# A two-layer hybrid block on one core: rests of split weights kept in DRAM, and the planner's price for a change of the array's shape

## The chip, the cores and the metric

The kernel runs on one core of a Trainium2 chip. The metric is the device time of one execution in microseconds, of which several runs are taken. A core has TensorE (PE in the profile, with its weight loads as PEld), VectorE (DVE), ScalarE (ACT), GpSimd (POOL) and SyncE (SP), which here issues all DMAs from one queue, in order.

## What is computed

Two layers over 1024 tokens of width 1024. Each layer has an input projection, three mixers side by side (an attention over the 256 best keys by an index score, an RWKV-7 recurrence, a sparse attention with compressed, selected and windowed keys), an output projection and a gated feed-forward network:

```python
for l in range(DEPTH):                       # DEPTH = 2, B = 1, T = 1024, D = 1024
    h = rms_norm(x, norm1_g[l]) * (1.0 + sc1) + sh1
    z = h @ w_in[l]
    ...
    o_a, o_b, o_c = dsa_mixer(...), rwkv7_mixer(...), nsa_mixer(...)
    mixed = jnp.concatenate([o_a, o_b, o_c], axis=-1) @ w_out[l]
    x = x + g1 * mixed
    h = rms_norm(x, norm2_g[l]) * (1.0 + sc2) + sh2
    gate, up = jnp.split(h @ ffn_wi[l], 2, axis=-1)
    x = x + g2 * ((jax.nn.silu(gate) * up) @ ffn_wo[l])
```

sh1, sc1, g1, sh2, sc2, g2 are six vectors of a linear map of the condition c (tensor `ada_w`). All is float32.

## The kernel before

The tokens are worked on in two halves of 512 (h = 0 and 1). A stage D(l, h) is the input projection of layer l for half h, a stage F(l, h) its output projection and feed-forward network; the main stream runs D00, D01, F00, D10, F01, D11, F10, F11 (the digits are l and h). The mixers' work runs beside them in streams of their own, and fills PE between the dense matmuls.

**Split weights.** PE multiplies in fp32r, and each product of float32 matrices is made of three: with weights and activations split into a rounded part and a rest, hi x hi, hi x lo and lo x hi (function `dense`, with activations named hh/hl, ohi/olo, acthi/actlo). A weight item is 128 partitions x 512 columns, 256 KB: four blocks of 128x128, so 12 matmuls over 512 tokens (a few items, of `wo`, have half of it). `Feed` hands the items out: 50 for a D stage, 152 for an F stage, 808 in all. For each, SP loads `wraw`, ACT rounds it to `whi`, and POOL subtracts to give the rest, `wlo` (`split`). Both halves of the tokens use the same weights, and both load and split them anew. `Feed.ahead` keeps two items split and up to two raw ones loaded. The tiles wraw, whi and wlo come from one pool of eight slots (`w=8`).

In this kernel's slots a raw load takes the slot of the raw item two before it, which comes free when POOL has subtracted that one; whi and wlo take the slots of the item three before, free when PE has done its last matmul on them.

**The order.** Nothing is scheduled while the kernel runs. `trace` is run once to record all operations with their dependences (`Program.add`); `Program.order` then places them one by one on the five engines by a table of costs (`Chip`), always the operation that can start first, and of several that are ready on one engine the one that was recorded first. Engines run their lists in the order that this gives. PE has one more rule: its 128x128 array can also work as smaller arrays ("shapes", counted in units of 32 rows and 32 columns, the full one being (4, 4)). `Chip.is_part` tells only full from partial; if the next matmul is of the other kind than the one before, and one of the same kind is ready that was recorded at most LATER = 100 operations after it, that one goes first. `Chip.start` and `Chip.put` price a change from full to partial with 0.095 + 0.05 us and one back with 0.045 + 0.105 us, and a change between two partial shapes with nothing.

On SP, DMAs go out in the planned order, each after the waits of its own; one that waits holds up all behind it.

Each instruction shows in the profile at L697, where `Program.issue` emits it, so tiles rather than lines tell operations apart. S, po, Y, X and at are tiles of the mixers: S, Y and X of the RWKV units, at and po of attention. z, k, v, r, low, dg, inv and Tt in DMAs are tiles that RWKV units pass through DRAM.

Of the kernel before, what the change touches and what calls it, by code (L numbers as in the profile page):

```python
# [13 lines left out]
F32 = mybir.dt.float32  # L14
# [483 lines left out]
class Rec:  # L498
    __slots__ = ("key", "name", "a", "k", "cost", "deps", "n", "users", "pe", "func", "port", "prio")
# [21 lines left out]
class Program:  # L521
# [32 lines left out]
    def add(self, key, name, a, k, aps, outs, cost, pe=None, port=False):  # L554
# [3 lines left out]
        r.prio = self.weave.cur.prio  # L558
# [46 lines left out]
    def order(self):  # L605
# [5 lines left out]
        kinds, begun = ([], []), set()  # L611
# [11 lines left out]
        while len(out) < len(recs):  # L623
            best = None
            for e in ENGINES:
                t = chip.free[e]
                if not ready[e]:
                    if not coming[e]:
                        continue
                    t = max(t, coming[e][0][0])  # L630
                while coming[e] and coming[e][0][0] <= t:
                    n = heapq.heappop(coming[e])[1]
                    heapq.heappush(ready[e], n)
                    if e == "PE":
                        heapq.heappush(kinds[Chip.is_part(recs[n])], n)
                n = ready[e][0]
                if e == "PE" and Chip.is_part(recs[n]) != chip.part:
                    same = kinds[chip.part]
                    while same and same[0] in begun:
                        heapq.heappop(same)  # L640
                    if same and same[0] - n <= LATER:
                        n = same[0]
                s = max(chip.start(recs[n]), at[n])
                if s > t + 0.1 and recs[n].port:

                    for m in heapq.nsmallest(8, ready[e])[1:]:
# [56 lines left out]
class Chip:  # L703
# [5 lines left out]
    def __init__(self):  # L709
        self.free = {e: 0.0 for e in ENGINES}  # L710
        self.cells = [[0.0] * 4 for _ in range(4)]
        self.part, self.first = False, False
        self.port, self.wire, self.table, self.ring = 0.0, 0.0, None, [0.0] * 8
        self.stretch, self.work, self.over, self.slow, self.lost = 0, 0.0, 0.0, False, 0.0

    @staticmethod
    def is_part(r):
        rows, cols, _ = r.pe
        return rows[1] - rows[0] + cols[1] - cols[0] < 8

    def start(self, r):

        t = self.free[r.key]
        if r.key == "PE":
            rows, cols, _ = r.pe
            part = self.is_part(r)
            for i in range(*rows):
                t = max(t, max(self.cells[i][cols[0]:cols[1]]))
            return t + (0.0 if part == self.part else 0.095 if part else 0.045)
# [4 lines left out]
    def put(self, r, s):  # L734

        if r.key == "PE":
# [6 lines left out]
            part = self.is_part(r)  # L743
            more = 0.105 if not part and self.first else 0.0

            step = c if not part or r.a[1].dtype != F32 else c / 2 + (0.0 if self.first else 0.05)
            if part and cols[1] - cols[0] == 1:
                step = 0.014
            self.first = part
# [8 lines left out]
            self.part = part  # L758
# [32 lines left out]
def trace(ctx: ExitStack, tc: tile.TileContext, A, out, layers=L, plan=None, program=None):  # L791
# [34 lines left out]
    def nm(s):  # L826
        cnt[0] += 1
        return f"{s}_{cnt[0]}"
# [101 lines left out]

    class Feed:


        def __init__(self, items):
            self.items, self.raw, self.split = list(items), [], []

        def load(self, n):
            while len(self.raw) < n and self.items:
                src, w, *led = self.items.pop(0)
# [5 lines left out]
                self.raw.append((raw, w, bool(led)))  # L945

        def ahead(self, n=AHEAD):
            self.load(1)
            while len(self.split) < n and self.raw:
                raw, w, led = self.raw.pop(0)  # L950
                self.split.append(split(raw, w, "w", G))
# [1466 lines left out]
    feed = Feed([i for k, l, h in seq for i in (items_D(l, h) if k == "D" else items_F(l, h))])  # L2418
# [106 lines left out]
```

## Time and profile before

| | us |
|---|---|
| median of 3 runs | 3439.8 |
| lowest and highest of them | 3438.86, 3444.59 |
| the profiled execution | 3442.73 |
| its span in the trace | 3441.0 |
| PE busy | 3215.3 |
| DVE busy | 2176.2 |
| ACT busy | 1775.1 |
| POOL busy | 1488.3 |

The busy time of an engine is the union of its instructions' times. Matmuls are pipelined: one of 512 columns is shown as some 0.4 us long, and the next one starts 0.23 us later. Where an engine sat idle, the view of waits names what ended the idle time. The stages overlap at their edges; here a stage is taken to begin when ACT splits its first weight item.

### The profile page before, as it was taken

To read this page: it belongs to the slowest core of one execution; us is meant where nothing else is said; L and a number is where in the kernel's file an instruction comes from. 1 tells how busy PE (TensorE), PEld (TensorE's weight loads), DVE (VectorE), ACT (ScalarE), POOL (GpSimd) and SP (SyncE) were. 2 spreads that over 40 slices of the span, in tenths; PEclk is the share of its full clock that TensorE was granted. 3 is DMA by queue.
4 is the path that set the end of the run, shared out by engine and by line. 5 is a ranking of instruction groups with operands and counts; after the bars stand their busy time and mean duration, and the time that the engine had idled before them with its cause. 6 is when DMAs were issued, how large, how long until landed. Compare 5 with 4: busy or idle time off the path is not lost. (4 is left out here: it accounts for less than half of the span.)

```text
span 3441.0 us, 58566 instructions
## 1 busy us (share of the span) xinstructions
PE 3215.3 (93%) x20564; PEld 2496.7 (73%) x20564; DVE 2176.2 (63%) x5705; ACT 1775.1 (52%) x3706; POOL 1488.3 (43%) x1235
## 2 busy tenths in 40 slices
PE   6898999989999998889899999899799999999999
PEld 3656776767767776767678887677577787778887
DVE  4688988898899634698952114698888853241112
ACT  3445566756674643545464234567777454343232
POOL 2433453434335444442434554443343344445554
PEclk8999999989999998999899999899999999999999
DMA  8684345445523243554223333463232222423333
GB/s 280 197 260 124 108 138 160 145 138 161 194 77 108 70 131 113 154 157 118 74 67 115 98 97 114 145 189 122 67 86 67 84 80 80 144 91 96 98 95 98
DMA packets 354755, 424.99 MB, mean 124 GB/s; under 512 B 129686, under 2 KB 167190, under 8 KB 354460
## 3 DMA queue, kind: packets, MB, share of 16 engines
q1 hardware_dynamic: 354460, 421.25, 39.9%
q8 instruction: 162, 2.65, 0.3%
q14 instruction: 133, 1.09, 0.1%
HBM read 347.06 MB, written 60.44 MB: 118 GB/s over the span
## 5 line engine op out<-in xcount | busy, mean ns | idle before, releaser
L697 POOL TENSOR_TENSOR wlo<-wraw,whi 128x512 fp32r<-128x512 f32 (+1 forms) x808 | 1072.1, 1329 | 1346.1 <-ACT whi L697 1243.1
L697 ACT ACTIVATE whi<-wraw 128x512 fp32r<-128x512 f32 (+1 forms) x808 | 500.7, 622 | 993.9 <-PE mm L697 664.6
L697 PE MATMUL mm<-hh,whi 128*128 128x512 f32 x2144 | 865.9, 405 | 38.5 <-ACT hh L697 10.4
L697 PE MATMUL mm<-hh,wlo 128*128 128x512 f32 x2128 | 847.9, 399 | 5.5 <-POOL wlo L697 5.4
L697 PE MATMUL mm<-hl,whi 128*128 128x512 f32 x2112 | 843.7, 400 | 5.5 <-DVE hl L697 3.2
L697 PEld LDWEIGHTS mm<-hh,whi 128*128 128x128 f32 x2144 | 410.5, 192 | 141.2 <-issue 16.1
L697 PEld LDWEIGHTS mm<-hh,wlo 128*128 128x128 f32 x2128 | 407.1, 191 | 101.0 <-POOL wlo L697 10.1
L697 PEld LDWEIGHTS mm<-hl,whi 128*128 128x128 f32 x2112 | 404.3, 191 | 94.6 <-issue 8.2
L697 DVE TENSOR_TENSOR sg<-sg,mm 128x512 f32<-128x512 f32 x87 | 59.5, 684 | 474.0 <-PE mm L697 473.8
L697 DVE SCALAR_TENSOR_TENSOR x<-mm,mod,x 128x512 f32<-128x512 f32 x232 | 172.9, 747 | 245.5 <-PE mm L697 244.5
L697 PE MATMUL mm<-acthi,whi 128*128 128x512 f32 x704 | 280.4, 402 | 13.9 <-DVE x L697 5.8
L697 PE MATMUL mm<-actlo,whi 128*128 128x512 f32 x704 | 277.6, 397 | 1.9 <-POOL actlo L697 1.8
L697 PE MATMUL mm<-acthi,wlo 128*128 128x512 f32 x704 | 276.6, 396 | 0.0
L697 ACT ACTIVATE p<-p,nb,rst 128x512 f32<-128x512 f32 (+3 forms) x256 | 170.6, 667 | 62.0 <-DVE nb L697 60.7
L697 ACT ACTIVATE junka<-score,tk_nt 128x512 int8<-128x512 f32 x240 | 165.9, 691 | 21.5 <-DVE tk_nt L697 16.0
L697 PEld LDWEIGHTS mm<-acthi,whi 128*128 128x128 f32 x704 | 133.3, 190 | 49.8 <-DVE x L697 6.8
L697 ACT COPY pT<-pt 128x512 f32<-128x512 f32 (+2 forms) x220 | 121.8, 588 | 70.3 <-PE pt L697 50.4
L697 PEld LDWEIGHTS mm<-actlo,whi 128*128 128x128 f32 x704 | 133.4, 190 | 31.2 <-POOL actlo L697 6.7
L697 PEld LDWEIGHTS mm<-acthi,wlo 128*128 128x128 f32 x704 | 133.5, 190 | 27.4 <-issue 0.2
L697 DVE TENSOR_SCALAR p<-p,rs 128x512 f32<-128x512 f32 (+3 forms) x288 | 151.9, 579 | 1.5 <-issue 0.9
L697 PE MATMUL pt<-c_ident,p 128*128 128x128 f32 x816 | 134.9, 282 | 14.3 <-DVE p L697 6.7
L697 PEld LDWEIGHTS pt<-c_ident,p 128*128 128x128 f32 x816 | 100.9, 143 | 48.8 <-issue 11.8
(386 smaller groups left out, 5916.7 us busy)
## 6 DMA issues: line engine op xcount, KB each, us to landing
wraw<-in_wi_dram SPq DMA_DIRECT2D x352, 256.0 KB, 2.6
ada<-in_ada_dram SPq DMA_DIRECT2D x192, 256.0 KB, 4.4
wraw<-in_win_dram SPq DMA_DIRECT2D x184, 256.0 KB, 3.2
wraw<-in_wo_dram SPq DMA_DIRECT2D x160, 256.0 KB, 2.6
x<-x SPq DMA_DIRECT2D x64, 256.0 KB, 3.7
w<-in_w_dram SPq DMA_DIRECT2D x64, 256.0 KB, 3.8
wraw<-in_wout_dram SPq DMA_DIRECT2D x64, 256.0 KB, 2.8
o_in<-o SPq DMA_DIRECT2D x32, 256.0 KB, 3.5
```

The lines of the kernel that those rows point to most:

```text
L697: getattr(engines[r.key], r.name)(*[real(x) for x in r.a], **{n: real(x) for n, x in r.k.items()})
```

## The change

Two things change.

First, `Feed` keeps the rests of three pairs of stages: ("D", 0), ("F", 0) and ("D", 1). In the first half's stage (D00, F00, D10) each wlo that POOL has made is also written to a DRAM tile of its own, by a DMA on SP. In the second half's stage (D01, F01, D11) the item's rest is loaded from there into a slot of the same pool, right behind its raw weights; ACT still rounds whi, and POOL subtracts nothing. F10 and F11 are as before. An item with a loaded rest counts twice in the limit of what is loaded ahead. There are 252 such items: 252 writes and 252 loads are new, and 252 of the 808 subtractions go. By the slots, a raw load of the second half's three stages now mostly takes the slot of the wlo four items before, which is free after PE's last matmul on it, and a load of a rest takes the slot of the raw item before, which is free after ACT's split.

Second, the planner tells the shapes of the array apart (`shape_of` in place of `is_part`): a change between any two shapes is priced with 0.095 us, and with 0.05 more on the first matmul in a partial shape or 0.105 on the first in the full one; and the rule of LATER now prefers a ready matmul of the very shape that PE is in.

```diff
-        kinds, begun = ([], []), set()
+        kinds, begun = {}, set()
...
-                        heapq.heappush(kinds[Chip.is_part(recs[n])], n)
+                        heapq.heappush(kinds.setdefault(Chip.shape_of(recs[n]), []), n)
                 n = ready[e][0]
-                if e == "PE" and Chip.is_part(recs[n]) != chip.part:
-                    same = kinds[chip.part]
+                if e == "PE" and Chip.shape_of(recs[n]) != chip.shape:
+                    same = kinds.get(chip.shape)
...
     @staticmethod
-    def is_part(r):
+    def shape_of(r):
         rows, cols, _ = r.pe
-        return rows[1] - rows[0] + cols[1] - cols[0] < 8
+        return rows[1] - rows[0], cols[1] - cols[0]
...
-            return t + (0.0 if part == self.part else 0.095 if part else 0.045)
+            return t + (0.0 if self.shape_of(r) == self.shape else 0.095)
...
-            part = self.is_part(r)
-            more = 0.105 if not part and self.first else 0.0
-
-            step = c if not part or r.a[1].dtype != F32 else c / 2 + (0.0 if self.first else 0.05)
+            shape = self.shape_of(r)
+            part, changed = shape != (4, 4), shape != self.shape
+            more = 0.105 if changed and not part else 0.0
+
+            step = c if not part or r.a[1].dtype != F32 else c / 2
+            if part and changed:
+                step += 0.05
...
+    KEPT = {("D", 0), ("F", 0), ("D", 1)}
...
         def load(self, n):
-            while len(self.raw) < n and self.items:
-                src, w, *led = self.items.pop(0)
+
+            while self.items:
+                (kind, l, h), src, w, *led = self.items[0]
+                if self.raw and sum(1 + (x[1] is not None) for x in self.raw) + 1 + (h and (kind, l) in KEPT) > n:
+                    break
+                self.items.pop(0)
                 raw = slot("wraw")
...
                 SY.dma_start(dst, src)
-                self.raw.append((raw, w, bool(led)))
+                key = lo = None
+                if (kind, l) in KEPT:
+                    key = src.tensor.name, src.offset
+                    if h:
+                        lo, key = slot("wlo", F32R), self.rests.pop(key)
+                        SY.dma_start(lo.bitcast(F32)[:, :w], key[:, :w])
+                self.raw.append((raw, lo, key, w, bool(led)))
...
-                raw, w, led = self.raw.pop(0)
-                self.split.append(split(raw, w, "w", G))
+                raw, lo, key, w, led = self.raw.pop(0)
+                if lo is not None:
+                    hi = slot("whi", F32R)
+                    S.activation(hi[:, :w], raw[:, :w], AF.Copy)
+                    self.split.append((hi, lo))
+                else:
+                    self.split.append(split(raw, w, "w", G))
+                    if key:
+                        t = self.rests[key] = dram(nm("rest"))
+                        SY.dma_start(t[:, :w], self.split[-1][1].bitcast(F32)[:, :w])
```

The planner puts the operations of all five engines in another order, nearly everywhere. Three places show what kind of change it is. The first is PE early in F01, before, where two RWKV units (S, Y: arrays of 64x64 and 128x64) and an attention block (po: 128x64) stand between dense matmuls (mm):

```order
L697 MATMUL mm_18411<-ohi_16782,wlo_18247 128x512
L697 MATMUL S_18154<-sh_18170,MT_18069 64x64 x2
L697 MATMUL po_17758<-pT_18369,tm_14168 64x256 x2
L697 MATMUL S_18332<-sh_18356,MT_18300 64x64 x2
L697 MATMUL S_18154<-sh_18170,MT_18069 64x64 x2
L697 MATMUL po_17758<-pT_18377,tm_14168 64x256 x2
L697 MATMUL Y_18448<-UV_17043,A_17115 64x64
L697 MATMUL Y_18448<-UV_17057,A_17131 64x64
L697 MATMUL S_18332<-sh_18356,MT_18300 64x64 x2
```

PE early in F01 after the change, with the same kinds of matmuls:

```order
L697 MATMUL mm_18929<-olo_17315,whi_18772 128x512
L697 MATMUL S_18945<-S_4853,MT_18846 64x64 x2
L697 MATMUL S_18640<-sh_18647,MT_18581 64x64 x2
L697 MATMUL po_18294<-pT_18871,tm_14346 64x256 x2
L697 MATMUL po_18294<-pT_18898,tm_14346 64x256 x2
L697 MATMUL S_18945<-sh_18952,MT_18846 64x64 x2
L697 MATMUL S_18640<-sh_18647,MT_18581 64x64 x2
L697 MATMUL mm_18929<-ohi_17207,wlo_18543 128x512
```

Matmuls of one shape from different units now stand together. The second place is SP late in D10, before:

```order
L697 DMA z10k_16948<-z_16901 128x512
L697 DMA k_16978<-z10k_16948 128x512
L697 DMA wraw_16983<-in_win_dram 128x512
L697 DMA wraw_17034<-in_win_dram 128x512
L697 DMA wraw_17053<-in_win_dram 128x512
L697 DMA z10v_17059<-z_17002 128x512
L697 DMA v_17099<-z10v_17059 128x4x64 x2
```

SP at the same place after the change:

```order
L697 DMA k_17215<-z10k_17180 128x512
L697 DMA rest_17225<-wlo_17202 128x512
L697 DMA wraw_17231<-in_win_dram 128x512
L697 DMA z10v_17234<-z_17198 128x512
L697 DMA v_17276<-z10v_17234 128x4x64 x2
L697 DMA rest_17292<-wlo_17245 128x512
L697 DMA wraw_17296<-in_win_dram 128x512
```

A write of a rest stands ahead of each raw load. The third is SP in F01, before, where w are weights of the compression and o results of attention:

```order
L697 DMA wraw_21181<-in_wi_dram 128x512
L697 DMA w_5429_21193<-in_w_dram 128x128
L697 DMA o_20606<-o_21191 128x128
L697 DMA o_20610<-o_21191 128x128
L697 DMA wraw_21219<-in_wi_dram 128x512
L697 DMA wraw_21237<-in_wi_dram 128x512
```

SP in F01 after the change, where an RWKV unit's Tt is loaded between:

```order
L697 DMA wraw_20123<-in_wi_dram 128x512
L697 DMA wlo_20126<-rest_9768 128x512
L697 DMA Tt_20118<-inv_414 64x8x64
L697 DMA wraw_20134<-in_wi_dram 128x512
L697 DMA wlo_20148<-rest_9821 128x512
L697 DMA wraw_20214<-in_wi_dram 128x512
L697 DMA wlo_20224<-rest_9922 128x512
```

Each raw load has the load of its rest behind it.

## Rows read from the trace of the kernel before

**Rows 1.** The page: the span, and busy time by engine.

```profile
span 3441.0 us, 58566 instructions
PE 3215.3 (93%) x20564; PEld 2496.7 (73%) x20564; DVE 2176.2 (63%) x5705; ACT 1775.1 (52%) x3706; POOL 1488.3 (43%) x1235
```

**Rows 2.** Windows: length, PE, PEld, DVE, ACT, POOL busy, clock, DMA share, GB/s.

```profile
34.80:311.50 276.70, 244.48 (x1562) 171.25 (x1562) 201.81 (x619) 128.01 (x277) 113.12 (x93) 0.93 0.68 209
311.50:662.30 350.80, 326.45 (x2686) 248.27 (x2684) 307.13 (x847) 218.12 (x494) 147.80 (x130) 0.97 0.46 135
662.30:1330.90 668.60, 629.16 (x4219) 487.49 (x4219) 499.02 (x1284) 392.12 (x845) 282.57 (x229) 0.97 0.41 127
1330.90:1551.50 220.60, 190.29 (x1043) 148.29 (x1043) 163.49 (x424) 105.17 (x212) 107.01 (x84) 0.92 0.48 143
1551.50:2127.10 575.60, 554.70 (x3761) 444.74 (x3760) 273.57 (x721) 248.77 (x495) 255.87 (x216) 0.98 0.32 97
2127.10:2357.90 230.80, 207.51 (x1112) 160.83 (x1111) 184.12 (x449) 145.01 (x309) 105.12 (x83) 0.93 0.51 157
...
3007.60:3441.00 433.40, 420.45 (x1876) 343.46 (x1876) 105.34 (x148) 141.76 (x236) 212.29 (x167) 0.99 0.30 96
```

**Rows 3.** Timeline of PE in F01: start us, us, engine, matmul, x count.

```profile
1612.19 0.45 PE L697 MATMUL S<-sh,MT 64*64 64x64 f32 x8
1612.57 0.65 PE L697 MATMUL po<-pT,tm 128*64 128x256 f32 x4
...
1613.27 0.33 PE L697 MATMUL S<-sh,MT 64*64 64x64 f32 x4
1613.53 0.33 PE L697 MATMUL Y<-UV,A 128*64 128x64 f32 x2
```

**Rows 4.** Waits of PE, 0 to 312 us: total us, times, longest.

```profile
PE mm L697 <- ACT whi L697: 3.8, 2, 2.3
PE mm L697 <- POOL wlo L697: 3.1, 2, 2.4
```

**Rows 5.** Waits of PE in D01, F01 and D11 (one view each).

```profile
PE X L697 <- DVE ex L697: 4.6, 1, 4.6
...
PE bc L697 <- DVE ex L697: 3.4, 2, 1.9
...
PE mm L697 <- DVE z L697: 6.4, 1, 6.4
PE mm L697 <- ACT whi L697: 4.0, 1, 4.0
```

**Rows 6.** Timelines of DVE and of POOL (last row), in D01.

```profile
484.20 0.75 DVE L697 SCALAR_TENSOR_TENSOR score<-rl,tm,score 128x512 f32<-128x512 f32 x1
...
485.93 1.15 DVE L697 TENSOR_SCALAR rx<-gv 128x8 f32<-128x8 f32 x1
487.00 1.86 DVE L697 SCALAR_TENSOR_TENSOR score<-rl,tm,score 128x512 f32<-128x512 f32 x1
...
485.77 2.54 POOL L697 TENSOR_TENSOR wlo<-wraw,whi 128x512 fp32r<-128x512 f32 x2 [3.14 <-ACT whi L697]
```

**Rows 7.** Feed: a group, timelines of POOL, SP and ACT, a DMA's landing.

```profile
L697 POOL TENSOR_TENSOR wlo<-wraw,whi 128x512 fp32r<-128x512 f32 (+1 forms) x808 | 1072.1, 1329 | 1346.1 <-ACT whi L697 1243.1
...
2999.77 0.33 SPq L697 DMA_DIRECT2D wraw<-in_wout_dram  x1
3300.70 1.29 POOL L697 TENSOR_TENSOR wlo<-wraw,whi 128x512 fp32r<-128x512 f32 x1 [1.42 <-ACT whi L697]
3302.02 14.01 SPq L697 DMA_DIRECT2D wraw<-in_wo_dram  x6
3302.71 0.63 ACT L697 ACTIVATE whi<-wraw 128x512 fp32r<-128x512 f32 x1 [2.09 <-PE mm L697]
3305.43 0.63 ACT L697 ACTIVATE whi<-wraw 128x512 fp32r<-128x512 f32 x1 [1.60 <-PE mm L697]
...
wraw<-in_wi_dram SPq DMA_DIRECT2D x352, 256.0 KB, 2.6
```

More of the change, by code (lines that the diff above doesn't have):

```diff
@@ L498 @@
 class Rec:
-    __slots__ = ("key", "name", "a", "k", "cost", "deps", "n", "users", "pe", "func", "port", "prio")
+    __slots__ = ("key", "name", "a", "k", "cost", "deps", "n", "users", "pe", "func", "port", "prio", "scope")
 def spread(offset, dims, unit):
@@ L557, in add @@
         r.n, r.deps, r.users = len(self.recs), set(), []
-        r.prio = self.weave.cur.prio
+        r.prio, r.scope = self.weave.cur.prio, self.weave.cur.scope
         r.func = a[2] if key == "S" and name == "activation" else None
@@ L711, in __init__ @@
         self.cells = [[0.0] * 4 for _ in range(4)]
-        self.part, self.first = False, False
+        self.shape = 4, 4
         self.port, self.wire, self.table, self.ring = 0.0, 0.0, None, [0.0] * 8
@@ L742, in put @@
                 self.stretch += 1
-            part = self.is_part(r)
-            more = 0.105 if not part and self.first else 0.0
-            step = c if not part or r.a[1].dtype != F32 else c / 2 + (0.0 if self.first else 0.05)
+            shape = self.shape_of(r)
+            part, changed = shape != (4, 4), shape != self.shape
+            more = 0.105 if changed and not part else 0.0
+            step = c if not part or r.a[1].dtype != F32 else c / 2
+            if part and changed:
+                step += 0.05
             if part and cols[1] - cols[0] == 1:
                 step = 0.014
-            self.first = part
             share = 1.0 if not part else (rows[1] - rows[0]) * (cols[1] - cols[0]) / 16.0
@@ L757, in put @@
                     self.cells[i][cols[0]:cols[1]] = [s + c + more] * (cols[1] - cols[0])
-            self.part = part
+            self.shape = shape
             self.free["PE"] = s + step + more
@@ L929, in drain @@
             pass
+    KEPT = {("D", 0), ("F", 0), ("D", 1)}
     class Feed:
         def __init__(self, items):
-            self.items, self.raw, self.split = list(items), [], []
+            self.items, self.raw, self.split, self.rests = list(items), [], [], {}
         def load(self, n):
-            while len(self.raw) < n and self.items:
-                src, w, *led = self.items.pop(0)
+            while self.items:
[3 more added lines that the diff above has]
+                self.items.pop(0)
                 raw = slot("wraw")
@@ L2417, in trace @@
                 seq.append(("D", l + 1, h))
-    feed = Feed([i for k, l, h in seq for i in (items_D(l, h) if k == "D" else items_F(l, h))])
+    feed = Feed([(s, *i) for s in seq for i in (items_D(*s[1:]) if s[0] == "D" else items_F(*s[1:]))])
     PR = dict(**{} or dict(index=1, topk=0, cmp=2, att=2, rw=3, rw2=4, lora=2, mod=7, main=8))
```

## The prediction

> **What bounds the kernel now.** I read the page first, then the windows by stage, then PE's waits stretch by stage, then the timelines of single engines. [rows 1] has PE busy for 3215.3 of 3441.0 us, DVE for 2176.2, ACT for 1775.1 and POOL for 1488.3. [rows 2] splits this by stage (order of the work: D00, D01, F00, D10, F01, D11, F10, F11; F10 is left out). In each stage PE is short of the stage's length by little: 32 us in D00, 24 in D01, 39 in F00, 30 in D10, 21 in F01, 23 in D11, 13 in F11. POOL is never above half of a stage, so the 252 subtractions that the change takes from it don't bound anything by themselves. DVE is 307 of 351 us in D01 and 184 of 231 us in D11: there it is nearly as full as PE. The granted clock (a mean of its two levels, 2.4 and 1.2 GHz) falls to 0.92 or 0.93 in D00, D10 and D11, the stages in which PE has the largest share of gaps. So the kernel is bound by PE's own sequence of instructions, with small gaps that mostly other engines make, and a term counts if it shortens PE's sequence or one of these gaps.
>
> A rule of the Trainium skill speaks against this reading. "Perfetto Trace Analysis", section "Identifying the Most-Contended Engine", says that matmul busy time doesn't tell how near TensorE is to its limit, and that the busy share of LDWEIGHTS (and MFU) does. By it PE would have 27% of room [rows 1], and a shorter PE sequence would give nothing: that is the second rival below. The trace bears it out only in part: F11 holds hardly anything but dense matmuls back to back, and there the weight loads are 343 of 433 us, 79% [rows 2], so 73% over the run leaves far less room than 27%.
>
> **Shape pricing (planner).** Counted over the whole PE order of both kernels, the array's shape changes 918 times before and 823 times now: 85 of the 95 that go are changes between two partial shapes (266 to 181), ten are between a partial and the full one (652 to 642). The price is in [rows 3]: eight records of S from 1612.19 to the po at 1612.57 take 0.38 us, four from 1613.27 to the Y at 1613.53 take 0.26. Four more cost 0.12, so the four alone are 0.12 and entering the new shape costs 0.14 us. 95 x 0.14 = 13 us, on PE, which is the path: **-13**. The bounds: 0, if the saved time turns into waits, and -26, if each change that goes also spares the partial matmuls next to it as much again by letting more of them run side by side. The order that PE now keeps holds back an urgent matmul of another shape, at most while matmuls of the current shape remain within 100 recorded operations; I give that nothing, since the pairs held back in the order shown are some 0.1 us each, and what it costs if many are held back is a part of the second rival.
>
> **Subtractions that go, second half.** 252 of the 808 POOL operations wlo go (50 in D01, 152 in F01, 50 in D11), 252 x 1.33 us = 335 us of POOL [rows 7]. Two things can reach PE. First the feed: the longest wait of PE for weights in these stages is 4.0 us for whi, in D11 [rows 5]. POOL has less queued ahead of what it still does, so I take **-3** of these 4; bounds 0 and -4. Second DVE: [rows 6] shows POOL running two wlo from 485.77 to 488.31, and beside them the DVE operation rx on 128x8 took 1.15 us and one of score 1.86, where score took 0.75 just before without POOL. About 2.1 us of DVE were lost to 2.5 us of POOL. DVE gets up to 335 x 0.8 = 270 us back in three stages, but most of it is idle time anyway. On the path are only PE's waits for DVE there, of which the longest in each stage are 4.6, 3.4 and 6.4 us [rows 5], 14 us together. I take half, **-7**, since not all of them have POOL beside them; bounds 0 and -14.
>
> **Rests written, first half.** Each split of D00, F00 and D10 adds a DMA of 256 KB on SP that waits for the same POOL wlo as the next raw load, and stands ahead of it (the order shows it). Behind the waiting write stand this raw load and the small transfers of z, k, v and low; but before the change the raw load itself waited there for the same operation, so no new event is waited for. What is new: 0.33 us to issue [rows 7], and the write's own transfer, 0.85 us for 256 KB at the 307 GB/s that 209 GB/s at a share of 0.68 make [rows 2], of which 0.33 run beside the issue of the raw load. So a raw load lands up to 0.85 us later. In dense stretches [rows 7] it is issued at 3302.02, just after the wlo that ended at 3301.99, lands 2.6 us later, at 3304.6, and is split at 3305.43: 0.8 us in hand, just eaten up. Beyond that split weights lie ready in two buffers ahead. So only items that PE waits for already cost anything: two waits for whi and two for wlo in D00 [rows 4], 4 x 0.85: **+3**. Bounds: 0, and +25 as in the first rival.
>
> **Rests loaded, second half.** Another 252 DMAs of 256 KB. From the slots of the pool of eight: a raw load now waits for PE's last matmul on the rest four items back, where it waited for POOL's subtraction two items back; a load of a rest waits for ACT's split of the item before. Behind that one on SP stand the next raw load and, in F01, the Tt and inv transfers of the rw units. An item is 12 matmuls, and in F11 ACT's splits follow each other every 2.72 us, from 3302.71 to 3305.43 [rows 7]. PE ends item j-4 at 0; rest j is issued by some 1.3, lands at 1.3 + 2.6 + 0.85 = 4.8, and is needed after three items, at 8.2. 3.4 us are left, about as before: **0**. Issuing takes 252 x 0.33 = 83 us of SP in 1157 us of the three stages, hidden while SP's queue is not late; without that cover each late load would cost PE up to 0.85 us.
>
> **The sum.** 3442.7 (the profiled execution) - 13 - 3 - 7 + 3 = 3422.7. That execution is 2.9 us above the median of the three runs, 3439.8, so on the median's scale 3420 us, 0.6% less. A measurement of this kernel can tell some 0.2% (7 us) from no change.
>
> **Rivals.**
> *Slower: the split loop of the first half becomes longer than PE's item.* The loop is: raw lands, ACT splits, POOL subtracts, the next raw but one is issued. From [rows 7] it is 0.1 + 0.63 + 0.1 + 1.29 + 0.03 + 2.6 = 4.75 us for two items, and PE needs 2 x 2.72 = 5.44. The write adds 0.85 to 1.2 (with its issue and transfer end to end): 5.6 to 5.95, which is 0.1 to 0.25 us an item over. It decides as soon as the write delays the raw load by more than 0.7 us while PE has nothing but dense work. For it: DMA share of 0.68 in D00. Against it: items of the first half take 276.7/50 = 5.5, 668.6/152 = 4.4 and 220.6/50 = 4.4 us on average [rows 2], with other matmuls between. If 100 to 252 of the 252 items ran at dense pace at 0.25 it costs 25 to 63 us in place of the 3 above: 3420 + 22 to 60, so 3442 to 3480; around 3460, 0.16.
> *No change: saved PE time becomes waits.* PE's gaps wait for chains through DVE and ACT, and moved instructions arrive earlier and wait longer. Then -13 and -7 are lost and 3420 + 20 = 3440; within 0.2% either way, 0.19.
> *More than forecast.* Beside the gaps, the clock is lost: (1 - 0.93) x 276.7 + (1 - 0.92) x 220.6 + (1 - 0.93) x 230.8 = 53 us in D00, D10 and D11 [rows 2]. If fewer changes (-26 by its far bound) and fewer DVE stalls close gaps, a quarter of the clock loss comes back, -13: 3420 - 13 - 13 = 3394; 0.18.
> *DMA becomes the bound.* The change adds 252 transfers out and 252 in, 130 MB. D00 has 0.32 x 276.7 = 89 us of DMA time free, and its 13 MB need 43 at 307 GB/s, so this should hide; if it doesn't, 3420 + 43 = 3463. 0.03. The Trainium skill leans to this case: "SBUF — State Buffer", section "A bandwidth-pool intuition that's wrong (but worth ruling out)", calls HBM almost always the end-to-end bottleneck; the trace, with 0.30 to 0.68 of the DMA engines busy [rows 2], shows no stage where it is.
> That the change doesn't do what it says is excluded by the order, which holds the 252 writes, the 252 loads and 252 fewer subtractions.
>
> **How the numbers follow.** Forecast 0.44, between 3402 and 3432; more than forecast 0.18; no change 0.19; slower 0.16 + 0.03. The range that leaves out a tenth at each side runs from 3390 (in the case of more) to 3456 (in the slower one). Faster by over 0.2%: 0.44 + 0.18 = 0.62; within 0.2%: 0.19; slower: 0.19.
>
> **What would show it.** Right: about 95 fewer changes seen as shorter runs of S, po and Y on PE; POOL at some 1150 us busy; DVE busy less by 30 us or more with the same instructions; no wait of PE for whi or wlo over 10 us in D00, F00 and D10 together; PE busy 10 to 20 us lower. Wrong: ACT's whi waiting for raw loads in F00 far longer than before (the first rival), PE idle time up by what its busy time fell (the second), or the granted clock lower in D00 or D10, which would take more than any term here.

## The result, and the profile after

The changed kernel takes **3468.1 us** (median of 4 runs, 3458.6 to 3470.1) where the kernel before took 3441.1 us beside it (3438.9 to 3444.6): a ratio of 1.0072, interval 1.0056 to 1.0089. It is slower by 27 us. The forecast was 20 us faster, and its range ended at 3456. The profiled execution took 3470.1 us.

The page of the changed kernel, span and busy time by engine, and the row of the DMA queue (packets, MB, share of 16 engines):

```profile
span 3468.3 us, 59225 instructions
...
PE 3210.9 (93%) x20564; PEld 2491.9 (72%) x20564; DVE 2067.0 (60%) x5705; ACT 1775.4 (51%) x3706; POOL 1156.5 (33%) x983
...
q1 hardware_dynamic: 427036, 551.30, 51.5%
```

Against [rows 1] PE is busy for 4 us less, DVE for 109 us less and POOL for 332 us less. The work that the change was meant to take off DVE and POOL went away, and the span is 27 us longer. So PE's idle time grew, from 3441.0 - 3215.3 = 226 us to 257 us. Where, the windows of the changed kernel tell, in the columns of [rows 2]; the rows are D00, D01, F00, D10, F01 and D11:

```profile
36.20:323.00 286.80, 243.19 (x1557) 169.53 (x1558) 207.48 (x626) 128.99 (x278) 113.01 (x93) 0.93 0.77 244
...
323.00:687.90 364.90, 328.18 (x2676) 251.15 (x2676) 281.30 (x876) 227.19 (x523) 74.68 (x80) 0.94 0.56 166
...
687.90:1355.60 667.70, 628.21 (x4240) 487.05 (x4238) 475.27 (x1246) 383.11 (x813) 278.62 (x228) 0.97 0.59 186
...
1355.60:1576.00 220.40, 187.66 (x996) 145.58 (x995) 149.09 (x417) 104.98 (x209) 104.54 (x84) 0.92 0.65 202
...
1576.00:2145.80 569.80, 547.06 (x3794) 439.86 (x3794) 253.81 (x730) 250.25 (x502) 62.53 (x63) 0.98 0.56 167
...
2145.80:2385.90 240.10, 211.85 (x1090) 163.44 (x1091) 159.12 (x473) 145.47 (x315) 38.53 (x34) 0.94 0.66 203
```

D00 is 10 us longer than in [rows 2], D01 14 and D11 9; F01 is 6 us shorter, F00 and D10 are as they were. PE's idle time (length less PE) went from 32 to 44 us in D00, from 24 to 37 in D01 and from 23 to 28 in D11; it is the idle time that makes D00 and D01 longer. In D01 DVE is busy for 26 us less and POOL for 73 less than before, and in this comparison that stage lost most. The last two columns are what rose in all six stages: the share of the DMA engines (0.46 to 0.56 in D01, 0.32 to 0.56 in F01) and the GB/s. A warning on the stages: the two kernels run different orders, and the new prices alone, without a rest, already make D01 10 us longer (360.6 us) and D10 10 us shorter (210.8 us). Which stage the rests lengthen is read further down, from kernels that differ by the rests alone; there it is D10 and D00.

What PE waits for in the changed kernel (whole run; total us, times, longest us):

```profile
PE mm L697 <- ACT whi L697: 19.2, 15, 3.5
PE mm L697 <- POOL wlo L697: 19.1, 14, 4.0
```

Before, the same two were 9.0 us (4 times) and 5.4 us (7 times). Adding every row of this view that names whi, wlo, a raw load or a rest, PE waited 22 us for weights before and 56 us after, of some 220 and 250 us of waits in all. For DVE it waits less than before (102 us in place of 116). The split that makes whi waits in turn. ACT's waits for raw loads, of the kernel before:

```profile
ACT whi L697 <- DMA wraw<-in_win_dram: 129.3, 52, 8.2
...
ACT whi L697 <- DMA wraw<-in_wo_dram: 62.9, 33, 4.8
ACT whi L697 <- DMA wraw<-in_wi_dram: 55.6, 25, 6.4
```

and of the changed kernel:

```profile
ACT whi L697 <- DMA wraw<-in_wi_dram: 204.0, 107, 4.9
ACT whi L697 <- DMA wraw<-in_win_dram: 170.6, 75, 7.8
ACT whi L697 <- DMA wraw<-in_wo_dram: 123.9, 60, 6.9
```

248 us and 110 times have become 499 us and 242 times: the split that used to wait for a buffer (its idle time before PE's matmuls freed one was 664.6 us, now 451.6) more often waits for its data. Such a wait is not yet a loss: in F01 these waits grew from 24 to 170 us, and F01 is shorter. From issue to landing (count, KB each, median us), in the changed kernel, where the rows of 256 KB leave out the 8 rests of half an item:

```profile
wraw<-in_wi_dram SPq DMA_DIRECT2D x352, 256.0 KB, 2.7
rest<-wlo SPq DMA_DIRECT2D x244, 256.0 KB, 2.5
wlo<-rest SPq DMA_DIRECT2D x244, 256.0 KB, 3.0
ada<-in_ada_dram SPq DMA_DIRECT2D x192, 256.0 KB, 5.1
wraw<-in_win_dram SPq DMA_DIRECT2D x184, 256.0 KB, 3.8
```

wi took 2.6 before [rows 7], win 3.2 and ada 4.4: the median landing got longer by 0.1 to 0.7 us.

### The profile page after: what moved, and what is told of

It is laid out like the page before. It is cut to its first block, busy times and chain, and to the rows that moved or that the text cites. A ratio compares the mean times of both kernels' runs of the same rounds, so it can differ in the third digit from the quotient of the medians.

```text
span 3468.3 us, 59225 instructions
## 1 busy us (share of the span) xinstructions
PE 3210.9 (93%) x20564; PEld 2491.9 (72%) x20564; DVE 2067.0 (60%) x5705; ACT 1775.4 (51%) x3706; POOL 1156.5 (33%) x983
## 5 line engine op out<-in xcount | busy, mean ns | idle before, releaser
L697 POOL TENSOR_TENSOR wlo<-wraw,whi 128x512 fp32r<-128x512 f32 (+1 forms) x556 | 733.1, 1320 | 1056.1 <-ACT whi L697 935.4
L697 ACT ACTIVATE whi<-wraw 128x512 fp32r<-128x512 f32 (+1 forms) x808 | 500.9, 622 | 1033.0 <-PE mm L697 451.6
L697 POOL TENSOR_TENSOR actlo<-sg,acthi 128x512 fp32r<-128x512 f32 x44 | 57.8, 1314 | 338.9 <-ACT acthi L697 338.6
L697 DVE TENSOR_SCALAR p<-p,rs 128x512 f32<-128x512 f32 (+3 forms) x288 | 140.4, 539 | 0.6
```

Of the source, the lines that this page charges most:

```text
L697: getattr(engines[r.key], r.name)(*[real(x) for x in r.a], **{n: real(x) for n, x in r.k.items()})
```

## The experiments

Two theories stood against each other. The first ("feed theory" in the expectations): the rests are paid for, by their bytes or by what they do to SP's queue, and the pricing gains. The second ("order theory"): the planner, given new prices or new records, writes another order, and the 27 us are what that order costs. Every kernel here was run in five rounds beside the kernel before, whose median was between 3440 and 3443 us; where several are in one group, a table stands behind it.

### The two halves alone, and a control

The pricing without the rests, and the rests with the prices of before:

```diff
-    KEPT = {("D", 0), ("F", 0), ("D", 1)}
+    KEPT = set()
```

> The new prices of shape changes alone; no rest is kept (KEPT is empty), so feed and DMAs are as before. Two theories. Feed theory: the loss comes from the added DMAs, which delay the weights in the D stages (PE's waits for whi, wlo and raw weights rose from some 22 to some 53 us), and the pricing gains its 5 to 13 us: 3426 to 3436 us, PE's waits for weights 15 to 30 us. Order theory: the order that sticks to a shape holds back urgent matmuls and costs more than the changes saved: 3450 to 3465 us, with the waits for weights unchanged.

```diff
-            return t + (0.0 if self.shape_of(r) == self.shape else 0.095)
+            return t + (0.0 if part == self.part else 0.095 if part else 0.045)
...
-            if part and changed:
-                step += 0.05
...
+            self.first = part
```

> The kept rests alone, with the planner's old prices. Feed theory: 3465 to 3485 us (after, plus the 5 to 13 us that the pricing gives), PE's waits for weights 45 to 65 us. Order theory: 3430 to 3445 us, since the rests by themselves neither gain nor lose.

And the kernel before with nothing changed but one number of the planner, ACT's fixed cost, by 1 ns and by 2 ns. It computes the same with the same instructions; only the order is another (with 1 ns, over half of the operations in PE's list stand elsewhere):

```diff
-        return (0.16 if psum else 0.2) + n / 1200.0 + 0.09 * (len(aps) - 2), False
+        return (0.161 if psum else 0.201) + n / 1200.0 + 0.09 * (len(aps) - 2), False
```

> A control: the kernel before with the planner's cost of ScalarE operations 1 ns higher. Nothing else is changed, but the planner's order moves in over half of the rows of TensorE's list. Both theories expect no more than 0.3% either way, 3430 to 3451 us; how far it moves says what a new order alone can do, and so what the other differences are worth.

> A second control: the planner's cost of ScalarE operations 2 ns higher, nothing else. The first control, with 1 ns, came to 3450.9 us, 8 us over the kernel before. If the order before is an ordinary draw, this falls on either side of it, 3432 to 3452 us; if it is a lucky one, it is again over, 3446 to 3460 us. Then the pricing alone, 3450.9 us, costs nothing against an ordinary order, and the rests are to be reckoned from some 3450 us.

| kernel | median us | ratio to before, 95% |
|---|---|---|
| pricing alone | 3450.9 | 1.0025 [1.0011, 1.0039] |
| rests alone | 3488.3 | 1.0132 [1.0116, 1.0149] |
| before, ACT +1 ns | 3450.9 | 1.0023 [1.0010, 1.0036] |
| before, ACT +2 ns | 3438.3 | 0.9998 [0.9980, 1.0017] |

The rests alone cost 46 us, more than the whole change. The pricing alone costs 8 us, but so does a nanosecond that means nothing. So one kernel whose order is planned anew says little about an edit worth ten us. Its order is one draw out of many that the planner could have written as well; the draw has to be averaged out, or the order kept fixed.

### The rests, with the order kept fixed

The kernel before with its own order, into which the 252 writes of the rests are put on SP, each when the subtraction behind it has ended by the plan. Nobody reads these rests; subtractions and all else are as before:

```diff
+                if r.key == "D":
+                    while held and held[0][0] <= self.starts[r.n]:
+                        lo = held.pop(0)[1]
...
+                        nc.sync.dma_start(t[:, :w], bass.AP(tensor=h, offset=lo.offset, ap=lo.ap))
...
+                if stage.get(r.n) in [('D', 0, 0), ('F', 0, 0), ('D', 1, 0)]:
+                    held.append((self.starts[r.n] + r.cost, r.a[0]))
```

> The kernel before with its own order of all engines unchanged, and only the 252 writes of rests put into SP's list, each ahead of the first DMA that the planner had starting after the rest was made. The second half still subtracts on POOL and loads no rest. Feed theory: the writes alone lengthen D00 by 8 to 15 us and D10 by 2 to 8, F00 by under 5: 3452 to 3468 us. Order theory (the loss is that the planner, which reckons with the added DMAs, arrives at a worse order): under 3 us, 3440 to 3446 us.

The same order with bytes alone: behind each of the 252 raw loads of D01, F01 and D11 a copy of the same 256 KB from DRAM to DRAM, which waits for no engine and is read by none:

```diff
+                if stage.get(r.n) in [('D', 0, 1), ('F', 0, 1), ('D', 1, 1)]:
+                    t = pools["dram"].tile([128, HF], F32, name=f"spare{seen}")
...
+                    nc.sync.dma_start(bass.AP(tensor=t.tensor, offset=0, ap=r.a[0].ap), real(r.a[1]))
```

> The kernel before with its own order unchanged, and in D01, F01 and D11 behind each raw load a copy of the same 256 KB within DRAM, which nobody waits for and whose landing frees nothing. It is the loads' issue on SP and their share of the DMA engines without what waits for them; POOL still subtracts. Feed theory: DMA share and issue time alone delay the weights, D01 and D11 get 3 to 10 us longer each, F01 under 3: 3450 to 3465 us. Rival: traffic is hidden, and the loss in D01 and D11 comes from the loads' place in SP's queue and from their waits: 3440 to 3446 us.

Both again with 16 of the 128 partitions, 32 KB in place of 256, and the writes once more with ACT issuing them, so that SP's queue is as before:

```diff
-                        nc.sync.dma_start(t[:, :w], bass.AP(tensor=h, offset=lo.offset, ap=lo.ap))
+                        ap = [[lo.ap[0][0], 16]] + [list(x) for x in lo.ap[1:]]
+                        nc.sync.dma_start(t[:16, :w], bass.AP(tensor=h, offset=lo.offset, ap=ap))
```

> As the 252 writes in the order of before (3499 us), but each write moves 16 of the 128 partitions: 32 KB in place of 256 KB, the same number of DMAs at the same places in SP's list with the same waits. If the bytes set the loss (each transfer takes some 0.85 us of all DMA engines from the loads beside it), some seven eighths of the 57 us go: 3445 to 3455 us. If SP's queue sets it (issuing takes 0.33 us or more of an in-order queue, and holds up what stands behind), nearly all stays: 3485 to 3500 us.

> As the 252 copies behind the raw loads of D01, F01 and D11 in the order of before (3499 us), but each copies 16 of 128 rows, 32 KB in place of 256 KB. If the bytes set the loss: 3445 to 3455 us. If SP's queue does: 3485 to 3500 us.

```diff
-                if r.key == "D":
+                if r.key == "S":
...
-                        nc.sync.dma_start(t[:, :w], bass.AP(tensor=h, offset=lo.offset, ap=lo.ap))
+                        nc.scalar.dma_start(t[:, :w], bass.AP(tensor=h, offset=lo.offset, ap=lo.ap))
```

> As the 252 writes of 256 KB in the order of before (3499 us), but ACT issues them, each ahead of its first operation that the planner had starting after the rest was made; SP's list is that of before. If SP's queue sets the loss: 3445 to 3465 us, with ACT some 0.1 to 0.4 us later per write. If the bytes set it: 3485 to 3505 us.

| kernel | median us | over before | ratio, 95% |
|---|---|---|---|
| 252 writes of 256 KB on SP | 3499.0 | +57 | 1.0173 [1.0150, 1.0196] |
| 252 copies of 256 KB on SP | 3498.6 | +57 | 1.0169 [1.0143, 1.0196] |
| 252 writes of 32 KB on SP | 3467.8 | +26 | 1.0084 [1.0063, 1.0105] |
| 252 copies of 32 KB on SP | 3450.7 | +9 | 1.0034 [1.0019, 1.0048] |
| 252 writes of 256 KB, issued by ACT | 3498.7 | +57 | 1.0167 [1.0146, 1.0188] |

Here the order of every engine is the one of before, and 252 transfers that nobody waits for cost 57 us, 0.23 us each, in the first half and in the second alike; neither theory had expected that much. With an eighth of the bytes 31 of the 57 us of the writes go, and 48 of the 57 of the copies. So a little over half of the price of the writes, and most of that of the copies, goes with the size of the transfer (the packets fall with the bytes, from some 140 to 32 a transfer, and no run tells the two apart). What is left of the writes, 26 us, is more than what is left of the copies, 9 us; the writes wait for POOL in SP's queue, and the copies don't. The last row takes the writes out of SP's queue and nothing is gained, but it proves less than it seems: there ACT issues the writes and waits for 48 us until earlier writes have landed and for 38 us on POOL (14 before), so one price may have been put in place of another.

The windows show that the price is paid where the bytes are. Of the writes, D00, F00 and D10:

```profile
34.50:330.00 295.50, 249.84 (x1562) 173.44 (x1562) 200.59 (x619) 128.23 (x277) 111.06 (x93) 0.91 0.75 240
...
675.30:1378.00 702.70, 638.78 (x4223) 489.97 (x4222) 495.34 (x1284) 390.66 (x844) 279.47 (x229) 0.95 0.55 176
...
1378.00:1611.60 233.60, 191.68 (x1041) 148.02 (x1040) 162.85 (x424) 105.01 (x211) 106.91 (x84) 0.92 0.62 192
```

Of the copies, D01, F01 and D11:

```profile
317.30:697.00 379.70, 339.25 (x2676) 257.23 (x2675) 305.62 (x845) 218.51 (x495) 146.26 (x130) 0.92 0.53 158
...
1577.00:2162.30 585.30, 555.27 (x3761) 443.97 (x3760) 272.23 (x721) 248.80 (x496) 255.27 (x216) 0.97 0.53 162
...
2162.30:2413.30 251.00, 209.93 (x1117) 162.17 (x1116) 184.38 (x449) 145.83 (x309) 104.15 (x83) 0.93 0.63 193
```

| stage | DMA share before | length before | with the bytes | us per transfer |
|---|---|---|---|---|
| F01 (copies) | 0.32 | 575.6 | 585.3 | 10/152 = 0.06 |
| F00 (writes) | 0.41 | 668.6 | 702.7 | 34/152 = 0.22 |
| D01 (copies) | 0.46 | 350.8 | 379.7 | 29/50 = 0.58 |
| D10 (writes) | 0.48 | 220.6 | 233.6 | 13/50 = 0.26 |
| D11 (copies) | 0.51 | 230.8 | 251.0 | 20/50 = 0.40 |
| D00 (writes) | 0.68 | 276.7 | 295.5 | 19/50 = 0.38 |

The stages with no new bytes stay within 7 us of before. Each length is from one profiled execution. Where the DMA engines were a third busy, a transfer costs little; in the other stages, at 0.41 to 0.68, it costs 0.22 to 0.58 us of the kernel, and not in the order of the share. No stage's mean gets above 0.75, but a mean hides full stretches. Two stretches of 10 us in D00, before and with the writes:

```profile
190.00:200.00 10.00, 6.75 (x42) 1.78 (x34) 6.54 (x29) 2.78 (x5) 3.18 (x4) 0.90 1.00 341
...
205.00:215.00 10.00, 3.51 (x12) 0.48 (x11) 7.11 (x28) 1.39 (x3) 2.54 (x3) 0.66 1.02 379
```

Of the stretches of 10 us in D00, 7 of 27 are at a share of 0.90 or more before, and 9 of 29 with the writes; there the DMA engines are full for a part of the time. (SP, whose DMAs use eight semaphores in turn, also waits there for the landing of the DMA eight places before: 39 times and 11 us before, 61 times and 16 us with the writes.) In D01 with the copies it is none of 37, and a transfer cost most there. D01 also shows how a gap is paid for twice: of its 29 us, 16 are new idle time of PE (24 to 40 us) and 13 are PE's own work (326.45 to 339.25 us for as good as the same instructions), at a granted clock that fell from 0.97 to 0.92, that is, with more of the stage at 1.2 in place of 2.4 GHz.

Who is late? In the kernel with writes ACT waits for the raw loads of wi 52 times (25 before):

```profile
ACT whi L718 <- DMA wraw<-in_win_dram: 162.1, 62, 10.2
ACT whi L718 <- DMA wraw<-in_wi_dram: 119.3, 52, 6.0
```

and SP waits for POOL with its raw loads and with its writes (lines 718 and 717 of that kernel):

```profile
SPq L718 <- POOL wlo L718: 1183.3, 471, 19.5
SPq L717 <- POOL wlo L718: 391.5, 165, 10.9
```

Together 1575 us; the raw loads alone waited 1586 us before. So the writes added no waiting for POOL, as the prediction said: they stand where the raw load would have waited. What they added lies behind that wait.

Since PE's order is the one of before, each matmul can be set against itself. Its delay grows in jumps: in D00, F00 and D10 there are 63 of more than 0.3 us, 68 us together, and others give a little back. The largest is in F00. The place before:

```profile
953.81 0.63 ACT L697 ACTIVATE Qhi<-Q 128x512 fp32r<-128x512 f32 x1 [4.28 <-DMA Q<-q01C]
...
960.35 0.63 ACT L697 ACTIVATE whi<-wraw 128x512 fp32r<-128x512 f32 x1 [2.31 <-DMA wraw<-in_wo_dram]
...
962.02 1.40 PE L697 MATMUL po<-pT,tm 128*64 128x256 f32 x9 [1.04 <-ACT pT L697]
```

and with the writes, of which one is the restwlo on SP:

```profile
988.29 0.63 ACT L718 ACTIVATE Qhi<-Q 128x512 fp32r<-128x512 f32 x1 [6.79 <-DMA Q<-q01C]
...
992.20 1.01 SPq L717 DMA_DIRECT2D restwlo<-wlo  x1
993.31 0.38 SPq L718 DMA_DIRECT2D wraw<-in_wo_dram  x1
...
997.39 0.63 ACT L718 ACTIVATE whi<-wraw 128x512 fp32r<-128x512 f32 x1 [5.99 <-DMA wraw<-in_wo_dram]
...
998.45 1.54 ACT L718 COPY pT<-pt 128x512 f32<-128x512 f32 x3
...
999.06 2.40 PE L718 MATMUL po<-pT,tm 128*64 128x256 f32 x10 [4.81 <-ACT pT L718]
```

PE's attention (po) waits 4.81 us in place of 1.04, and its row names ACT's pT. But pT stands in ACT's list behind the split whi, the split waits for its raw load, the raw load stands on SP behind a write, and further back another transfer, Q, is late as well. So a late raw load reaches PE through other work of ACT, in a row of PE's view that names no weight.

The rival that put the loss on the write standing ahead of the raw load has a run of its own: the changed kernel with each write recorded behind the raw load.

```diff
+            late = []
...
-                        t = self.rests[key] = dram(nm("rest"))
-                        SY.dma_start(t[:, :w], self.split[-1][1].bitcast(F32)[:, :w])
+                        late.append((key, self.split[-1][1], w))
...
+            for key, lo, w in late:
+                t = self.rests[key] = dram(nm("rest"))
+                SY.dma_start(t[:, :w], lo.bitcast(F32)[:, :w])
```

> The changed kernel, with the write of a rest recorded behind the raw load that waits for the same subtraction, so that it stands behind it on SP. Feed theory in the form of the split loop (the write ahead of the raw load makes it land late): D00 and D10 get back most of what they lost, 8 to 15 us: 3450 to 3460 us. If bandwidth and the eight DMAs in flight set the delay, not the order of these two, it stays at 3463 to 3473 us.

It took 3493.3 us, 1.0151 [1.0127, 1.0175]: not better. The whole change in its three draws (below) takes 3468 to 3495, so it is inside what a new order makes of it, and no gain shows.

### The draw averaged out

Pricing alone, rests alone and the whole change again, each with ACT's planned cost 1 and 2 ns higher, as in the controls:

> The new prices alone with ScalarE's planned cost 1 ns higher: the third draw of an order with the new prices (3451 and 3425 so far; with the old ones 3442, 3451, 3438). If the pricing gains what the changes of shape are worth, some 13 us, the mean of its three draws lies near 3431, and this one at 3415 to 3435. If it gains nothing, the mean is 3444 and this one 3436 to 3460.

> The new prices alone, no rests, with the planner's cost of ScalarE operations 2 ns higher: a second draw of an order made with the new prices. The first draw took 3450.9 us; the two controls with the old prices took 3450.9 and 3438.3, the kernel before 3442. If the pricing is worth the 13 us that I gave it, this falls to 3425 to 3435; if it is worth nothing, it lies in the spread of the others, 3436 to 3453.

> The kept rests with the old prices, ScalarE's planned cost 1 ns higher. The same order without rests took 3451. If the rests cost 46 us: 3480 to 3505. If their first draw was an unlucky order: 3450 to 3470.

> The kept rests with the old prices, ScalarE's planned cost 2 ns higher. The same order without rests took 3438. If the rests themselves cost what their first draw showed against its pair, 46 us: 3475 to 3495. If that draw was an unlucky order: 3440 to 3465.

> The whole change with ScalarE's planned cost 1 ns higher. If rests cost some 40 us and the pricing gives back some 10, it is 3465 to 3485; if rests cost under 20, 3440 to 3460.

> The whole change with ScalarE's planned cost 2 ns higher; the pricing alone with that cost took 3425. If the rests cost 17 us as between the first draws of the pricing with and without them (3451 and 3468): 3435 to 3450. If the first draw of the pricing alone was unlucky and the rests cost 40 or more, as with the old prices: 3460 to 3480.

| median us | +0 | +1 ns | +2 ns | mean |
|---|---|---|---|---|
| neither | 3442 | 3450.9 | 3438.3 | 3444 |
| pricing alone | 3450.9 | 3433.7 | 3425.4 | 3437 |
| rests alone | 3488.3 | 3499.3 | 3467.1 | 3485 |
| both | 3468.1 | 3495.0 | 3489.3 | 3484 |

The six pairs that differ by the rests alone are +46, +48 and +29 at the prices of before and +17, +61 and +64 at the new ones: always slower, by 41 and 47 us on average. The pairs that differ by the pricing alone are +9, -17 and -13 without the rests and -20, -4 and +22 with them: -7 and -1 on average, and of both signs. The 27 us that were measured for the change are the luckiest of its three draws; on the means it is 40 us slower.

The same pairs tell the stage. What the rests add to the length of each, in us (one profiled execution of each kernel):

| the pair | D00 | D01 | F00 | D10 | F01 | D11 |
|---|---|---|---|---|---|---|
| prices of before, +0 | +13 | +8 | +3 | +15 | -6 | +14 |
| prices of before, +1 ns | +12 | -3 | +21 | +22 | -13 | +4 |
| prices of before, +2 ns | +9 | +4 | +10 | +25 | -14 | 0 |
| new prices, +0 | +9 | +4 | -3 | +10 | -12 | +4 |
| new prices, +1 ns | +17 | +3 | +5 | +23 | +1 | +1 |
| new prices, +2 ns | +15 | +10 | +12 | +19 | -13 | +16 |
| mean | +12 | +5 | +8 | +19 | -10 | +7 |

The stages that write rests, D00, F00 and D10, grow by 40 us on average, D00 and D10 in every pair. The stages that load them come out at +2 together: F01 gains 10 us, and D01 and D11 lose 11. (With a stage taken to begin at its first matmul on PE, the sums are 43 and -1.) So in an order that is planned with the rests, nearly the whole loss is made where they are written. PE's busy time on the page goes both ways: the pricing takes 16 us off it without the rests and 10 with them (means of the three draws), and the rests add 15 and 21 for the same matmuls.

Pricing alone with +2 ns, 0.9955 [0.9940, 0.9970], is faster than both kernels, by some 16 us against before; how much of that is the pricing and how much the draw, three draws don't tell.

### The long stages alone

The rests of F00 alone are kept, 152 items of 252, with the new prices; without and with +2 ns:

```diff
-    KEPT = {("D", 0), ("F", 0), ("D", 1)}
+    KEPT = {("F", 0)}
```

> Both parts, but rests kept only for the feed-forward stages of layer 0 (F00 writes, F01 loads); D00, D01, D10 and D11 feed as before. Feed theory: the loss sits in the D stages, where the DMA engines are 0.56 to 0.77 busy; without them 3425 to 3440 us, and F01 keeps the 6 us that it won. If the writes and loads cost the same per item everywhere, 152 of 252 items remain and the loss is some 0.6 of the whole: 3455 to 3462 us. Order theory: as with the pricing alone, 3450 to 3465 us.

> New prices and rests kept for F00 and F01 alone, ScalarE's planned cost 2 ns higher; the pricing alone with that cost took 3425. If the loss of the rests sits in the D stages and F01 gains: 3420 to 3432. If rests cost the same per item everywhere (152 of 252 items, 40 us for all): 3440 to 3455.

3455.8 us (1.0041 [1.0027, 1.0056]) and 3449.1 us (1.0023 [1.0012, 1.0034]). Against pricing alone in the same draw that is +5 and +24. The second was run to see whether the D stages carry the whole loss, in which case it would have come out at 3420 to 3432; they don't. On average 152 items cost 14 us, 0.10 each, and the other 100 the rest of the 47, some 0.3 each: the same leaning to the D stages as in the table of the pairs, from two draws only. Against pricing alone F00 is 11 and 18 us longer, and F01 12 and 10 us shorter.

## Why the prediction was wrong, step by step

- **Rests written +3: here it failed.** The stages that write rests grew by 40 us on the mean of six pairs (D00 12, F00 8, D10 19); writes alone in an order that did not know of them cost 57. The step priced a delayed raw load at 0.85 us and let it count only where PE already waited for weights, four items, since "0.8 us in hand" and two buffers ahead would cover the others. Two things in it were wrong. The cover was read in one dense place of F11 [rows 7] and taken for all stages. It is there where the split waits for a buffer that PE frees, as in F01 before:

```profile
ACT whi L697 <- PE mm L697: 191.6, 109, 2.4
...
ACT whi L697 <- DMA wraw<-in_wo_dram: 16.1, 9, 2.8
```

In D00 before, 17 of the 50 splits wait for their raw load itself, so nothing is in hand there:

```profile
ACT whi L697 <- DMA wraw<-in_win_dram: 56.5, 17, 8.2
...
ACT whi L697 <- PE mm L697: 7.8, 5, 3.7
```

In D10 it is 36 us, 17 times, for raw loads against 11 us, 5 times, for PE. And it counted only PE's waits for weights, where a late raw load also holds up all that stands behind its split in ACT's list, as the largest jump shows. That this holds for most of the jumps is not shown; ACT's waits for transfers of all kinds were 409 us before, 543 with the writes and 712 after.
- **Rests loaded 0:** not far off as a net. The stages that load come out at +2 us, where -10 was foretold for feed and DVE; whether the loads cost some 12 us or the gains did not come, no run tells. SP now waits for PE's matmuls for 269 us and for ACT's splits for 127 (26 and 5 before), by the new slots; copies of the same bytes in the old order, with all subtractions kept, cost 57.
- **"so this should hide" failed with it.** The share free in a stage, 0.32 in D00, was used as if the bytes could be put there. They cost 0.38 us each in D00 and 0.22 in F00, where more than half of the DMA time was free. The rival "DMA becomes the bound" (3463, chance 0.03) was the nearest in its time. The Trainium skill leans its way too: "SBUF — State Buffer", section "A bandwidth-pool intuition that's wrong (but worth ruling out)", calls HBM almost always the end-to-end bottleneck. No run here tells HBM from the DMA engines. As a bound of a whole stage neither shows: no stage of after is above a mean share of 0.77, and PE is still busy for 93%. In D00 the DMA engines are full for a part of the time, in D01 hardly, and bytes cost in both.
- **The split-loop rival** named the side, and a range that holds the result. Its sign came: ACT's whi waited for raw loads in F00 for 94 us in place of 49. But the place is another: F00, where 152 of its 252 items are, is as long as before (667.7 and 668.6 us) and loses 8 us on the mean of the pairs, D00 and D10 with 100 items lose 31; and with the raw load ahead of the write nothing is won. In the kernel with writes put into the old order F00 did lose 34 us, so a delayed feed is part of it there; bytes with no write ahead of any raw load cost as much.
- **Shape pricing -13: mechanism seen, gain not settled.** The changes of shape went from 918 to 823 as counted, 835 with pricing alone, and PE's busy time by 4 us in place of the 10 to 20 foretold, since the rests add to it: the pricing alone takes 16 us off it on the mean of three draws (8 to 22). In time it is -7 us on that mean, with single draws from +9 to -17, and -1 with the rests: part of the saved time became waits, as the rival of no change had it.
- **DVE beside POOL -7:** the busy times came as said, POOL 1156.5 for "some 1150" and DVE 109 us less. Only F01 is shorter, by 6 us here and by 10 on the mean of the pairs; in D01 and D11 DVE's busy time fell and the stage grew. PE's waits for DVE fell by 14 us over the whole run, but in D01, F01 and D11 together, where the term was priced, they rose from 33 to 38.
- **Feed of the second half -3:** the longest wait for whi in D11 fell from 4.0 [rows 5] to 3.5 us, but all waits for whi there rose from 4.0 to 7.3 us, waits for raw loads and rests of 10 us came beside them, and PE's waits for weights as a whole rose by 34.
- **What would show it:** the sign "no wait of PE for whi or wlo over 10 us in D00, F00 and D10 together" was a poor one: the kernel before, with 9 us in D00 and 1 in F00, stands at 10 already. After the change it is 15, 1 and 12. PE's waits in D00 in the changed kernel:

```profile
PE mm L697 <- POOL wlo L697: 8.1, 6, 3.9
...
PE mm L697 <- ACT whi L697: 4.1, 3, 1.8
...
PE tm L697 <- POOL wlo L697: 3.0, 2, 2.0
```

The first two are 12 us, against 7 us in [rows 4]; the third, which [rows 4] leaves out, was 2.2 us (2 times). The prediction gave four waits 0.85 us more, 3 us in all; the four became nine and 5 us more, and the stage grew by 10.

**Open** stays how the bytes' price divides among the chains: the largest jump is followed above, the others are not. In the kernel with writes no row of PE's view grew by more than some 8 us (po for ACT's pT, then whi and ada by 5), and a median landing of wi, win and ada grew by 0.1 to 0.4 us. There PE's waits for weights rose by 5 us only and all its waits by 46; in the changed kernel they rose by 34 and 31. Open too is how the price of the writes divides between SP and ACT as issuers, what the loads cost by themselves, and the pricing's gain below some 15 us.

## What to carry to other kernels

A transfer that nobody waits for is not free because the DMA engines have a third or a half of their time left: price its bytes against the chains that wait for other transfers in that stage, and test it first as bare traffic in the unchanged order, which is one short edit. Read that as an upper bound: in the old order the two halves' bytes cost 57 us each, and orders planned with the rests lost 41 to 47 us for both. Look for slack in the stage where the work is put: who ends the waits of the split there, its data or its buffer? Moving work from an engine that has slack (POOL at 43%) to bytes is a gain only if PE's gaps name that engine. Where a planner writes the order, run the kernel with a meaningless nudge of the planner two or three times before reading an edit's effect: here such nudges alone moved the time of the kernel before by -4 to +8 us, and three draws of the whole change lie 27 us apart.

## What the runs showed of the hardware that was not expected

- 256 KB that nobody reads cost 0.23 us of the kernel on average (57/252), from 0.06 us in a stage with the DMA engines at a mean share of 0.32 to 0.58 us in one at 0.46; its own transfer is 0.85 us by the prediction's estimate. The median landing of the neighbours rose little: wi 2.6 to 2.7 us, ada 4.4 to 4.8 with the writes.
- Two DMA issuers cost the same: 57 us with the writes on SP and 57 us with them on ACT, where ACT waited 48 us for landings of its own earlier writes.
- A mean share of 0.68 over D00 (277 us) hides 7 stretches of 10 us, of 27, in which the DMA engines are at 0.90 or more.
